# Index queries by halves of the tokens, two pairs of blocks that trade their counting engine, and a reordered start, in a two-layer decoder trunk

## The chip, the cores and the metric

The kernel runs on one core of one Trainium2 chip. The metric is the device time of one execution, in microseconds; the time shown is the median of several runs. Five engines matter: PE (TensorE), DVE (VectorE), ACT (ScalarE), POOL (GpSimd) and the sync queue SP, which issues nearly all DMAs.

## The reference

```python
# layer 0: sparse attention; layer 1: gated short convolution; each followed by a SwiGLU FFN
mod = silu(c) @ ada_w[i] + ada_b[i]                  # shifts, scales and gates, 6 x 1024
h = rmsnorm(x, norm1_g[i]) * (1 + sc1) + sh1
...
q, k, v, qi, ki, wi = split(h @ w_in)                # 16 heads, 4 kv heads, 8 index heads, dim 64
q, k = rope(rmsnorm(q)), rope(rmsnorm(k)); qi = rope(qi); ki = rope(layernorm(ki))
for each block of 128 queries:
    score = einsum(relu(einsum(qi, ki)), wi)         # summed over the 8 index heads
    score = where(causal, score, -inf)
    sel = top_k(score, 256)                          # 256 keys for every query
    p = softmax(q . k[sel] * scale); o = p . v[sel]
x = x + g1 * (o @ w_out)
x = x + g2 * swiglu(rmsnorm(x, norm2_g[i]) * (1 + sc2) + sh2)
```

1024 tokens, model width 1024, everything in float32. Blocks 0 and 1 (the first 256 queries) see at most 256 keys, so that only blocks 2 to 7 need scores and a selection.

## The kernel before

All instructions are recorded first and then ordered when the program is built: `Plan.drain` is a list scheduler. Each engine has a clock of its own; among the operations whose inputs are ready it issues the one with the lowest `pri`, which is a due time in microseconds set in the code that records the operation. `unit(s)` sets the due time `T_PROJ + s * SLOT` (45 + 6.2 s). Tiles with a tag live in rings, and a ring hands out its buffers in the order in which the program recorded them: a tile can't be had before the earlier tile in its buffer has been read for the last time. Each engine then runs its own list in order. All instructions are emitted at line 244, so that the rows below tell groups apart by tile names.

A product of float32 matrices is made of three matmuls on split operands: `split` makes a rounded high part (`whi`, `hhi`: a cast, on ACT mostly) and the remainder (`wlo`, `hlo`: a subtraction on DVE). `wpair` loads one pair of weight tiles (two `raw` loads of 512 KB) and splits it into the four units of the ring `whi`/`wlo`, four casts and four subtractions.

The start, `first_norm`: eight loads of x are transposed on PE into `xt`, through the PSUM ring `mm` of two banks. The shift and scale of layer 0 (`mod`, j = 0 and 1) come from 16 loads of 512 KB of `ada_w`, eight for each j (k = 0 to 7). Five eighths of each row block are summed on DVE (`ada_step`, tile `sc`), three eighths on PE (`ada_pe`): three one-column matmuls for a k, each k in a tile of its own of the ring `mm`, followed by a DVE addition into `mod`. The loads go to tiles `stage`, `raw` and `s4` (shown as `s`). `vectors` loads the small parameter vectors into rows, transposes them, and `ada_scale` needs its `norm1_g`. `rope_tables` needs its frequencies and makes C and S, which go through DRAM (`rd`). At the end `nz`, `hhi` and `hlo` are the normalized input.

`project`: KI (index key and weights) for both halves of 512 tokens; then the index queries QI: for each of two column pairs j, one `wpair`, and both halves (of half 0 only its last 256 tokens, as blocks 0 and 1 need none); `rope_pair` copies (`rt`), rotates (`sw`, `rt`) and writes to DRAM (`qid`). Then, for each block 2 to 7, `index` loads the block's queries back (`karena<-qid`), makes 4 x 2 score tiles on PE (`ps_L`), ACT takes their relu (`s`), and eight DVE operations add them up (`sc<-s,wiT,sc`). `select` finds the 256th largest score of two blocks at once bit by bit, 31 bits: a count of the scores above a trial value for each block (tile `junk`), then three small DVE operations on `bs`. The count is a Sign with an accumulator on ACT, or a compare with an accumulator on DVE. Before, blocks 2, 3 count on DVE, and 4, 5 and 6, 7 on ACT. The bits' due times run from the pair's start to `until[pair]`. `selected` then makes the block's mask `bias` by ten or so DVE operations. K, Q and V projections follow in the program (512-column matmuls into `mm`), and attention, `attend`, comes after the pools of the projection have been closed. It runs blocks 0 to 7 in turn, with the output projection and 48 more `ada_w` steps (`adaw`, `adacc`) between them.

Of the kernel before, what the change touches and what calls it, by code (L numbers as in the profile page):

```python
# [9 lines left out]
F32 = mybir.dt.float32  # L10
F32R = mybir.dt.float32r
BF16 = mybir.dt.bfloat16
# [3 lines left out]
ALU = mybir.AluOpType  # L16
# [434 lines left out]
P = 128  # L451
T = 1024
D = 1024
KT = D // P
TB = T // P
HW = 512
NH = 2
# [4 lines left out]
IH = 8  # L462
TOPK = min(256, T // 4)
FREE_BLK = TOPK // P
# [7 lines left out]
C_QI = C_V + KVH * HD  # L472
# [3 lines left out]
R_C, R_N1, R_N2, R_CW, R_G, R_IF = 0, 8, 24, 40, (64, 96), 66  # L476
# [6 lines left out]
def blk(b):  # L483
    return slice(b * P, (b + 1) * P)


class Trunk:
# [94 lines left out]
        nc.vector.tensor_tensor(out, r, t, op=ALU.mult)  # L582


    def setup(self, c, ada_b, arenas):
        nc, cp = self.nc, self.cp
        self.ident = ident = cp.tile([P, P], F32, name="ident")
        nc.gpsimd.memset(ident, 1.0)
        nc.gpsimd.affine_select(ident, ident, pattern=[[-1, P]], compare_op=ALU.is_equal,
                                fill=0.0, base=0, channel_multiplier=1)  # L590
        self.ones = cp.tile([P, 1], F32, name="ones")
        nc.vector.memset(self.ones, 1.0)
        self.blk4 = cp.tile([P, 4], F32, name="blk4")
        nc.vector.memset(self.blk4, 0.0)
        for i in range(4):
            nc.vector.memset(self.blk4[32 * i:32 * i + 32, i:i + 1], 1.0)
        rc, rowb = arenas[0].part_of(0)[0:8, P:2 * P], arenas[1].part_of(0)[0:96, 0:P]
        nc.sync.dma_start(rc, c.rearrange("o (k p) -> (o k) p", p=P))
        self.plan.pri = 1.2
        nc.sync.dma_start(rowb, ada_b.rearrange("l (k p) -> (l k) p", p=P))  # L600
        self.cact = cp.tile([P, 8], F32, name="cact")
        pv = self.ps("sm")
        nc.tensor.transpose(pv[:, 0:8], rc, ident[:8, :8])
        nc.scalar.activation(self.cact, pv[:, 0:8], AF.Silu)
        self.adab = cp.tile([P, 96], F32, name="adab")
        pb = self.ps("sm")
        nc.tensor.transpose(pb[:, 0:96], rowb, ident[:96, :96])
        nc.vector.tensor_copy(self.adab, pb[:, 0:96])
        mod = cp.tile([P, 2, 6, 8], F32, name="mod")
        self.mod = [[mod.part_of((i, j))[:, i, j] for j in range(6)] for i in range(2)]  # L610
        aff = cp.tile([P, 2, 2, 8], F32, name="aff")
        self.aff = [[aff.part_of((i, j))[:, i, j] for j in range(2)] for i in range(2)]

    def vectors(self, n1, n2, conv_w, gq, gk, lg, lb, rope_c, arenas, kgb):

        nc, cp = self.nc, self.cp
        rows = arenas[0].part_of(1)[:, 0:P]
        nc.vector.memset(rows, 0.0)
        for r0, n, v in ((R_N1, 16, n1.rearrange("l (k p) -> (l k) p", p=P)),
                         (R_N2, 16, n2.rearrange("l (k p) -> (l k) p", p=P)),  # L620
                         (R_CW, 24, conv_w.rearrange("o w (k p) -> (o w k) p", p=P)),
                         (R_IF, 1, rope_c)):
            nc.sync.dma_start(rows.part_of((1, r0))[r0:r0 + n, :], v)
        g = arenas[1].part_of(96)[96:98, 0:HD]
        for r, v in enumerate((gq, gk)):
            nc.sync.dma_start(g[r:r + 1], v)
        self.plan.pri = 1.15
# [6 lines left out]
        rd = [1] + [(1, r) for r in (R_N1, R_N2, R_CW, R_IF, *R_G)]  # L634
        nc.tensor.transpose(pv[:, 0:P], rows.part_of(rd), self.ident)
        nc.vector.tensor_copy(vec, pv[:, 0:P])
        self.plan.pri = 25.5
# [31 lines left out]
        if j in (1, 4) and c0 + n == KT or layer == 0 and j == 1:  # L669
            self.ada_scale(layer, j)  # L670

    def ada_pe(self, w, layer, j, k, d0, tag="mm"):


        n = w.free // P
        ps, dst, b0 = self.ps(tag), self.mod[layer][j][:, d0:d0 + n], layer * 48 + j * 8 + d0
        for d in range(n):
            self.nc.tensor.matmul(ps[:, d:d + 1], w[:, blk(d)], self.cact[:, k:k + 1],
                                  start=True, stop=True)
        self.nc.vector.tensor_tensor(dst, ps[:, 0:n], dst if k else self.adab[:, b0:b0 + n],  # L680
                                     op=ALU.add)

    def ada_scale(self, layer, j):

        n, r0 = (0, R_N1) if j == 1 else (1, R_N2)
        r0 += 8 * layer
        self.nc.vector.scalar_tensor_tensor(self.aff[layer][n], self.mod[layer][j], 1.0,
                                            self.vec[:, r0:r0 + 8], op0=ALU.add, op1=ALU.mult)

    def raw(self):  # L690
        return self.wp.tile([P, D], F32, name="raw", tag="raw")
# [76 lines left out]
def trunk_kernel(tc, x, c, positions, ada_w, ada_b, norm1_g, norm2_g, attn_w_in, attn_q_norm_g,  # L768
                 attn_k_norm_g, idx_k_ln_g, idx_k_ln_b, attn_w_out, conv_w_in, conv_w,
                 conv_w_out, ffn_w_gate, ffn_w_up, ffn_w_down, rope_c, out):  # L770
    plan = Plan(tc.nc, tc)
    with ExitStack() as ctx:
        ctx.enter_context(tc.manual_schedule())
        tk = Trunk(plan)
        for p in (tk.cp, tk.pp):
# [4 lines left out]
        a.first_norm(x, positions, lambda v: tk.setup(c, ada_b, v), lambda v: tk.vectors(  # L780
            norm1_g, norm2_g, conv_w, attn_q_norm_g, attn_k_norm_g, idx_k_ln_g, idx_k_ln_b,
            rope_c, v, a.score[2][:, 256:384]))
        a.project()
        a.attend()
# [22 lines left out]

class Attention:
    T_PROJ, SLOT = 45.0, 6.2
    ON_ACT = 4  # L810

    def __init__(self, tk, w, w_out, ada_w, xspill):
        self.tk, self.nc, self.w, self.w_out = tk, tk.nc, w, w_out
# [3 lines left out]
        def dram(name, shape):  # L817
# [19 lines left out]
        self.junk = [sel.tile([P, n], BF16, name="junk%d" % n) for n in (self.ON_ACT * P, T)]  # L837
# [13 lines left out]
    def first_norm(self, x, positions, setup, vectors):  # L851
# [9 lines left out]
        for tt in range(TB):  # L861
            plan.pri = 1.0 + tt
            h = tt // 4
# [4 lines left out]
            for i in range(2):  # L868
                ps = tk.ps()
# [8 lines left out]
            if tt % 4 == 3:  # L878
                bc = tk.norm_bc(ss.part_of(h)[:, 4 * h:4 * h + 4], sp, "L")[:, 0:HW]
                plan.pri = 5.0 + 4 * h  # L880
                for d in range(KT):
                    plan.tt(zs[h].part_of(d)[:, d], xT[h](d), bc, ALU.mult)
        plan.pri = 13.5
        vectors((self.C, self.S))
        for j in (1, 0):
            acc = self.score[5 + j][:, 0:5 * P]
            stage = self.hp.tile([P, 4, D], F32, name="stage%d" % j, tag="hi0" if j else "lo0")
            for k in range(KT):
                plan.pri = 10.0 + k + 8 * (1 - j)
                if k % 2:  # L890
                    w = stage.part_of(k)[:, k // 2]
                else:
                    w = self.s4() if k % 4 else tk.raw()
                last = nc.sync.dma_start(w, tk.ada_rows(self.ada_w, 0, j, k))
                plan.pri = 1.1
                tk.ada_step(w[:, 0:5 * P], k, acc)
                tk.ada_pe(w[:, 5 * P:], 0, j, k, 5)
            tk.ada_end(0, j, [acc])
        plan.pri = 28.5
        tk.rope_tables(positions, self.C, self.S, self.score[4:2:-1], self.rd)  # L900
        self.h = []
        for half in range(NH):
# [30 lines left out]
    def project(self):  # L933
# [13 lines left out]
            s += 1  # L947
        self.unit(s + 1)
        self.ki_chain(kw)
        for j in range(IH // 4):  # L950
            self.unit(s)
            w = tk.wpair(self.w, C_QI + j * 2 * P)
            for half in range(NH):
                ts = slice(max(0, FREE_BLK * P - half * HW), HW)
                ab, sl, s = self.rope_pair(w, half, ts, None, None, s)
                for two in range(2):
                    self.to_dram(ab[two], self.qid, j, two, half, sl)
        self.free_bias()
        t = s
        ends = []  # L960
        for n, b in enumerate(range(FREE_BLK, TB)):
            self.unit(t)
            self.index(b, n)
            t += 0.5
            if b % 2:
                self.unit(t)
                ends += self.select((b - 1, b), b >= self.ON_ACT)
        for pri, end, args in sorted(ends, key=lambda e: e[0]):
            plan.pri = pri
            end(*args)  # L970
# [25 lines left out]
        for b in range(TB):  # L996
            ps = tk.ps()[:, 0:KVH * HD]
            for k in range(KT):
                hi, lo = (v[:, blk(b % 4)] for v in self.h[b // 4](k))
                tk.mm3(ps, hi, lo, *w[k // 4](k % 4), k == 0, k == KT - 1)  # L1000
            plan.copy(self.vst.part_of(b)[:, b], ps)
            s += 0.5
            self.unit(s)

    def rope_pair(self, w, half, ts, col, ss, s):

# [102 lines left out]
    def index(self, b, n):  # L1109
# [1 line left out]
        wd = (b + 1) * P  # L1111
        q = self.karena.part_of((1 + n // 2, n % 2))[:, 1 + n // 2, half_of(n % 2)].rearrange(
            "p (h t) -> p h t", t=P)
        nc.sync.dma_start(q, self.qid[:, blk(b)].rearrange("(h p) t -> p h t", p=P))
        sc = self.score[b]
        for hp in range(IH // 2):
            rs = [self.s4()[:, 0:wd] for _ in range(2)]
# [720 lines left out]
```

## Time and profile before

| | us |
|---|---|
| median of 3 runs (2352.1 to 2356.06) | 2353.39 |
| the profiled execution | 2353.95 |
| its span in the trace | 2352.2 |

The profile and the trace show one execution. Times in rows are from the start of the span. 1.75 us of the execution's time lie outside the span.

### The profile page before, as it was taken

How to read it: one execution, taken by the hardware profiler on the slowest of the kernel's cores; microseconds unless marked ns; L12 is line 12 of the kernel's file. 1: busy time of each engine (PE TensorE's matmuls, PEld its weight loads, DVE VectorE, ACT ScalarE, POOL GpSimd, SP SyncE). 2: the span in 40 equal slices, each digit the busy share in tenths (PEclk: the TensorE clock that was granted, in tenths of full speed). 3: DMA queues.
4: the chain of work that ended last, by engine and by line, in shares of the span. 5: the costliest groups of instructions: out<-in, count | busy, mean ns of one | idle time of the engine just before them, and what ended most of it. 6: DMA issues, size and time to landing. Idle time of an engine off the chain costs nothing.

```text
span 2352.2 us, 32869 instructions
## 1 busy us (share of the span) xinstructions
PE 2263.6 (96%) x11743; PEld 1828.6 (78%) x11743; DVE 1887.3 (80%) x3858; ACT 1121.7 (48%) x2106; POOL 5.1 (0%) x19
## 2 busy tenths in 40 slices
PE   7999989999999999999999899999999999999999
PEld 6757866776797778888887677788878888888877
DVE  5789979686589888887699989886898766665996
ACT  4468989857754233333343552223553333333434
POOL 0000000000000000000000000000000000000000
PEclk7999999999999999999999999999999999999999
DMA  7414332322244756443944143334344222238343
GB/s 287 123 53 99 102 105 73 117 91 64 81 140 131 223 177 188 151 153 111 326 139 147 63 131 113 103 90 152 109 126 152 89 90 76 90 119 311 126 161 112
DMA packets 304078, 311.27 MB, mean 132 GB/s; under 512 B 15113, under 2 KB 208682, under 8 KB 303914
## 3 DMA queue, kind: packets, MB, share of 16 engines
q1 hardware_dynamic: 302474, 307.86, 41.1%
q8 instruction: 92, 1.51, 0.3%
q10 hardware_dynamic: 1440, 1.31, 0.2%
q14 instruction: 72, 0.59, 0.1%
HBM read 258.00 MB, written 51.12 MB: 131 GB/s over the span
## 4 chain that ended last, share of the span: by engine, by line
PE 74%; DVE 16%; DMA 6%; ACT 2%; issue 2%; SPq 0%; ACTq 0%; DVEq 0%
PE ps_g L244 38%; PE ps_mm L244 26%; PE ps_sm L244 5%; DVE u L244 2%; PE ps_L L244 2%; PE ps_o L244 2%; DVE wlo L244 2%; DVE sc L244 2%; DMA adaw<-in_ada_w_dram 2%; DVE v L244 2%; DVE s L244 2%; DVE xr L244 1%; ACT p L244 1%; DVE p L244 1%; DVE adacc L244 1%
## 5 line engine op out<-in xcount | busy, mean ns | idle before, releaser
L244 ACT CAST whi<-s 128x512 fp32r<-128x512 f32 x341 | 211.4, 621 | 457.9 <-PE ps_g L244 181.4
L244 PE MATMUL ps_g<-t,whi 128*128 128x512 f32 x1160 | 361.2, 392 | 3.8 <-ACT t L244 2.9
L244 ACT CAST whi<-raw 128x512 fp32r<-128x512 f32 (+1 forms) x271 | 165.9, 618 | 366.2 <-PE ps_g L244 145.5
L244 PE MATMUL ps_g<-h,whi 128*128 128x512 f32 x1080 | 333.9, 390 | 0.0
L244 DVE TENSOR_TENSOR wlo<-raw,whi 128x512 fp32r<-128x512 f32 (+1 forms) x288 | 195.8, 684 | 79.4 <-ACT whi L244 79.0
L244 PEld LDWEIGHTS ps_g<-t,whi 128*128 128x128 f32 x1160 | 218.3, 189 | 51.0 <-ACT t L244 3.3
L244 DVE TENSOR_TENSOR wlo<-s,whi 128x512 fp32r<-128x512 f32 x342 | 232.5, 684 | 26.4 <-ACT whi L244 25.8
L244 PEld LDWEIGHTS ps_g<-h,whi 128*128 128x128 f32 x1080 | 202.2, 188 | 41.6
L244 PE MATMUL ps_g<-t,wlo 128*128 128x512 f32 x580 | 227.6, 392 | 4.8 <-DVE wlo L244 4.7
L244 PE MATMUL ps_g<-ph,whi 128*128 128x512 f32 x660 | 207.6, 393 | 4.4 <-DVE ph L244 2.3
L244 PE MATMUL ps_g<-h,wlo 128*128 128x512 f32 x540 | 210.5, 390 | 0.0
L244 PE MATMUL ps_mm<-t,whi 128*128 128x512 f32 x632 | 198.9, 396 | 4.0 <-ACT whi L244 4.0
L244 PEld LDWEIGHTS ps_g<-ph,whi 128*128 128x128 f32 x660 | 125.3, 190 | 32.4 <-DVE ph L244 3.3
L244 PEld LDWEIGHTS ps_mm<-t,whi 128*128 128x128 f32 x632 | 120.8, 192 | 30.3 <-ACT whi L244 5.1
L244 PEld LDWEIGHTS ps_g<-t,wlo 128*128 128x128 f32 x580 | 109.4, 189 | 29.7 <-DVE wlo L244 7.1
L244 DVE CUSTOM_DVE_ANT_0 p<-ps_L,bias 128x512 f32<-128x512 f32 (+3 forms) x192 | 100.1, 551 | 38.9 <-PE ps_L L244 22.2
L244 PE MATMUL ps_g<-ph,wlo 128*128 128x512 f32 x330 | 130.5, 395 | 0.0
L244 PE MATMUL ps_mm<-t,wlo 128*128 128x512 f32 x316 | 125.3, 396 | 4.7 <-DVE wlo L244 4.6
L244 ACT ACTIVATE junk<-sc,bs 128x896 bf16<-128x896 f32 (+3 forms) x124 | 123.4, 995 | 8.4 <-DVE bs L244 6.6
L244 ACT ACTIVATE p<-p,nm,qsc 128x256 f32<-128x256 f32 (+7 forms) x128 | 113.2, 886 | 21.4 <-DVE nm L244 19.9
L244 DVE SCALAR_TENSOR_TENSOR adacc<-adaw,cact,adacc 128x512 f32<-128x512 f32 x140 | 104.4, 746 | 20.5 <-DMA adaw<-in_ada_w_dram 20.3
L244 PEld LDWEIGHTS ps_g<-h,wlo 128*128 128x128 f32 x540 | 101.4, 188 | 21.6 <-DVE wlo L244 0.4
(331 smaller groups left out, 4713.1 us busy)
## 6 DMA issues: line engine op xcount, KB each, us to landing
ph<-in_ffn_w_down_dram SPq DMA_DIRECT2D x88, 512.0 KB
adaw<-in_ada_w_dram SPq DMA_DIRECT2D x160, 256.0 KB
raw<-in_ffn_w_gate_dram SPq DMA_DIRECT2D x52, 512.0 KB
raw<-in_ffn_w_up_dram SPq DMA_DIRECT2D x52, 512.0 KB
rt<-hid SPq DMA_DIRECT2D x64, 256.0 KB
raw<-in_conv_w_in_dram SPq DMA_DIRECT2D x32, 512.0 KB
hid<-u SPq DMA_DIRECT2D x52, 256.0 KB
raw<-in_ffn_w_down_dram SPq DMA_DIRECT2D x44, 256.0 KB
```

The lines of the kernel that those rows point to most:

```text
L244: f(*[a.get() if isinstance(a, Ref) else a for a in args], **{k: a.get() if isinstance(a, Ref) else a for k, a in kw.items()})
```

## The change

Three groups of edits.

- Start: `norm1_g` is loaded with `c` and transposed with it, so that `ada_scale` for j = 1 needs no `vectors`; `vectors` is recorded after the `ada_w` steps, with the due time 28.5. `ada_pe` accumulates all eight k of a j in one PSUM bank of the ring `o`, and one DVE addition follows. The `ada_w` rows of j = 0 go to eight slots in the buffers that held x.
- Index queries: half 0 of both column pairs comes first, then half 1 of pair 1 (with the weights already there) and half 1 of pair 0, whose weights are loaded and split again. Blocks 2, 3 are indexed and their selection begun behind half 0; a block's query load depends on the parts of `qid` of its own half alone. A half of 256 columns counts for half a slot, so that all later due times of the projection are two slots (12.4) earlier.
- Counting: blocks 2, 3 and 6, 7 on ACT, 4, 5 on DVE.

```diff
-        rc, rowb = arenas[0].part_of(0)[0:8, P:2 * P], arenas[1].part_of(0)[0:96, 0:P]
-        nc.sync.dma_start(rc, c.rearrange("o (k p) -> (o k) p", p=P))
+        rc, rowb = arenas[0].part_of(0)[0:24, P:2 * P], arenas[1].part_of(0)[0:96, 0:P]
+        nc.sync.dma_start(rc[0:8], c.rearrange("o (k p) -> (o k) p", p=P))
+        nc.sync.dma_start(rc[8:24], n1.rearrange("l (k p) -> (l k) p", p=P))
...
-    def ada_pe(self, w, layer, j, k, d0, tag="mm"):
+    def ada_pe(self, w, k, ps):
         n = w.free // P
-        ps, dst, b0 = self.ps(tag), self.mod[layer][j][:, d0:d0 + n], layer * 48 + j * 8 + d0
         for d in range(n):
             self.nc.tensor.matmul(ps[:, d:d + 1], w[:, blk(d)], self.cact[:, k:k + 1],
-                                  start=True, stop=True)
-        self.nc.vector.tensor_tensor(dst, ps[:, 0:n], dst if k else self.adab[:, b0:b0 + n],
-                                     op=ALU.add)
+                                  start=k + d == 0, stop=k == KT - 1 and d == n - 1)
...
-        plan.pri = 13.5
-        vectors((self.C, self.S))
         for j in (1, 0):
             acc = self.score[5 + j][:, 0:5 * P]
-            stage = self.hp.tile([P, 4, D], F32, name="stage%d" % j, tag="hi0" if j else "lo0")
+            stage = [self.hp.tile([P, 4, D], F32, name="stage%d" % j, tag=tag)
+                     for tag in (("hi0",) if j else ("lo0", "lo1"))]
+            ps = tk.ps("o")
             for k in range(KT):
                 plan.pri = 10.0 + k + 8 * (1 - j)
-                if k % 2:
-                    w = stage.part_of(k)[:, k // 2]
+                if j == 0 or k % 2:
+                    w = stage[k // 4 if j == 0 else 0].part_of(k)[:, k % 4 if j == 0 else k // 2]
                 else:
                     w = self.s4() if k % 4 else tk.raw()
...
-                tk.ada_pe(w[:, 5 * P:], 0, j, k, 5)
+                tk.ada_pe(w[:, 5 * P:], k, ps)
+            nc.vector.tensor_tensor(tk.mod[0][j][:, 5:], ps[:, 0:3],
+                                    tk.adab[:, 8 * j + 5:8 * j + 8], op=ALU.add)
             tk.ada_end(0, j, [acc])
         plan.pri = 28.5
+        vectors((self.C, self.S))
...
-    ON_ACT = 4
+    ON_ACT, IDX = (2, 3, 6, 7), 0.5
...
-        for j in range(IH // 4):
+        ends = []
+        for half, j in ((0, 0), (0, 1), (1, 1), (1, 0)):
             self.unit(s)
-            w = tk.wpair(self.w, C_QI + j * 2 * P)
-            for half in range(NH):
-                ts = slice(max(0, FREE_BLK * P - half * HW), HW)
-                ab, sl, s = self.rope_pair(w, half, ts, None, None, s)
-                for two in range(2):
-                    self.to_dram(ab[two], self.qid, j, two, half, sl)
+            if (half, j) != (1, 1):
+                w = tk.wpair(self.w, C_QI + j * 2 * P)
+            ts = slice(max(0, FREE_BLK * P - half * HW), HW)
+            ab, sl, e = self.rope_pair(w, half, ts, None, None, s)
+            s += (e - s) * (ts.stop - ts.start) / HW
+            for two in range(2):
+                self.to_dram(ab[two], self.qid, j, two, half, sl)
+            if (half, j) == (0, 1):
+                ends += self.indexed(s, (2, 3))
         self.free_bias()
-        t = s
-        ends = []
-        for n, b in enumerate(range(FREE_BLK, TB)):
-            self.unit(t)
-            self.index(b, n)
-            t += 0.5
-            if b % 2:
-                self.unit(t)
-                ends += self.select((b - 1, b), b >= self.ON_ACT)
+        ends += self.indexed(s, (4, 5, 6, 7))
...
+    def indexed(self, t, blocks):
+        ends = []
+        for b in blocks:
+            self.unit(t)
+            self.index(b, b - FREE_BLK)
+            t += self.IDX
+            if b % 2:
+                self.unit(t)
+                ends += self.select((b - 1, b), b in self.ON_ACT)
+        return ends
...
-        nc.sync.dma_start(q, self.qid[:, blk(b)].rearrange("(h p) t -> p h t", p=P))
+        src = self.qid.part_of([(b // 4, j, two) for j in range(2) for two in range(2)])
+        nc.sync.dma_start(q, src[:, blk(b)].rearrange("(h p) t -> p h t", p=P))
```

## Rows read from the trace of the kernel before

**Rows 1.** Busy time of each engine by stretch: PE, PEld, DVE, ACT, POOL, clock, DMA

```profile
100.00:111.50 11.50, 11.50 (x55) 9.46 (x54) 5.63 (x11) 4.39 (x8) 0.00 (x0) 1.00 0.33 101
111.50:125.00 13.50, 10.28 (x45) 8.08 (x43) 4.66 (x7) 2.28 (x4) 0.00 (x0) 1.00 0.43 126
125.00:187.00 62.00, 60.62 (x270) 30.44 (x270) 58.69 (x125) 45.24 (x101) 3.03 (x5) 0.97 0.15 43
187.00:309.00 122.00, 121.97 (x702) 106.23 (x702) 115.05 (x438) 111.14 (x216) 0.29 (x1) 1.00 0.36 96
309.00:430.00 121.00, 107.02 (x896) 73.15 (x893) 99.66 (x384) 109.73 (x293) 0.00 (x0) 0.97 0.33 101
```

**Rows 2.** Chain that ended last, in order of time: start, us, what

```profile
107.81 3.68 PE ps_mm L244 x16
...
116.17 8.87 DMA karena<-qid
...
237.77 8.81 PE ps_mm L244 x38
...
308.98 4.39 DMA adaw<-in_ada_w_dram
...
339.37 0.81 ACT junk L244 x2
...
424.25 1.03 ACT junk L244 x2
```

**Rows 3.** Order of time in the start: start, us, engine, operation, [idle before]

```profile
25.23 0.83 PE L244 MATMUL ps_mm<-cact,raw 128*128 128x1 f32 x6
...
29.31 1.44 PE L244 MATMUL ps_mm<-cact,s 128*128 128x1 f32 x6 [2.41 <-DVE mod L244]
...
54.59 1.52 ACT L244 ACTIVATE nz<-zs,mod,aff 128x512 f32<-128x512 f32 x2 [1.67 <-DVE mod L244]
```

**Rows 4.** Busy time by stretch in the start, columns as in the first group

```profile
24.00:28.00 4.00, 2.70 (x21) 2.22 (x20) 3.71 (x6) 1.66 (x3) 0.00 (x0) 0.91 0.93 312
32.00:36.00 4.00, 4.00 (x21) 4.00 (x21) 1.42 (x9) 0.00 (x0) 0.00 (x0) 0.50 0.74 258
```

**Rows 5.** PE's busy time on tile ps_mm: stretch, length, busy (count), clock, DMA

```profile
111.50:125.00 13.50, 10.28 (x45) 1.00 0.43 126
125.00:140.00 15.00, 3.92 (x9) 0.89 0.25 71
140.00:160.00 20.00, 9.81 (x34) 1.00 0.09 28
160.00:187.00 27.00, 8.94 (x27) 1.00 0.13 39
```

**Rows 6.** Groups by shape, 0 to 330 us: count, busy us, mean ns, idle before

```profile
L244 PE MATMUL ps_L<-karena 64*128 64x512 f32 x96 | 26.2, 636 | 1.2 <-ACT s L244 1.0
...
L244 DVE TENSOR_TENSOR wlo<-raw,whi 128x512 fp32r<-128x512 f32 x36 | 24.4, 684 | 4.7 <-ACT whi L244 4.6
...
L244 ACT ACTIVATE junk<-sc,bs 128x768 bf16<-128x768 f32 x26 | 24.3, 936 | 0.5
...
L244 ACT ACTIVATE junk<-sc,bs 128x640 bf16<-128x640 f32 x26 | 21.5, 828 | 2.3 <-DVE bs L244 2.0
...
L244 DVE SCALAR_TENSOR_TENSOR sc<-s,wiT,sc 128x512 f32<-128x512 f32 x7 | 5.2, 739 | 0.1
...
L244 DVE SCALAR_TENSOR_TENSOR sc<-s,wiT,sc 128x384 f32<-128x384 f32 x7 | 4.3, 618 | 1.5 <-ACT s L244 1.0
...
L244 DVE TENSOR_SCALAR_CACHE_REDUCE junk<-sc 128x768 bf16<-128x768 f32 x1 | 0.9, 936 | 0.0
...
L244 DVE TENSOR_SCALAR_CACHE_REDUCE junk<-sc 128x640 bf16<-128x640 f32 x1 | 0.8, 812 | 0.0
```

**Rows 7.** Tile ps_L on PE, sum of the stretches from 57 to 309 us

```profile
sum 252.00, PE 36.53; mean PE 2.44
```

**Rows 8.** Tile ps_sm on PE, the same sum (160 matmuls)

```profile
sum 252.00, PE 19.48; mean PE 1.30
```

**Rows 9.** Tile junk (the counts), sum of stretches from 80 to 460 us

```profile
sum 380.00, DVE 47.55 ACT 132.49; mean DVE 2.50 ACT 6.97
```

**Rows 10.** Tile junk, sum of stretches from 300 to 700 us

```profile
sum 400.00, DVE 0.00 ACT 49.50; mean DVE 0.00 ACT 2.48
```

More of the change, by code (lines that the diff above doesn't have):

```diff
@@ L582, in rsqrt_small, with setup @@
         nc.vector.tensor_tensor(out, r, t, op=ALU.mult)
-    def setup(self, c, ada_b, arenas):
+    def setup(self, c, ada_b, n1, arenas):
         nc, cp = self.nc, self.cp
@@ L601, in setup @@
         self.cact = cp.tile([P, 8], F32, name="cact")
+        self.n1 = cp.tile([P, 16], F32, name="n1")
         pv = self.ps("sm")
-        nc.tensor.transpose(pv[:, 0:8], rc, ident[:8, :8])
+        nc.tensor.transpose(pv[:, 0:24], rc, ident[:24, :24])
         nc.scalar.activation(self.cact, pv[:, 0:8], AF.Silu)
+        nc.vector.tensor_copy(self.n1, pv[:, 8:24])
         self.adab = cp.tile([P, 96], F32, name="adab")
@@ L612, in setup, with vectors @@
         self.aff = [[aff.part_of((i, j))[:, i, j] for j in range(2)] for i in range(2)]
-    def vectors(self, n1, n2, conv_w, gq, gk, lg, lb, rope_c, arenas, kgb):
+    def vectors(self, n2, conv_w, gq, gk, lg, lb, rope_c, arenas, kgb):
         nc, cp = self.nc, self.cp
@@ L618, in vectors @@
         nc.vector.memset(rows, 0.0)
-        for r0, n, v in ((R_N1, 16, n1.rearrange("l (k p) -> (l k) p", p=P)),
-                         (R_N2, 16, n2.rearrange("l (k p) -> (l k) p", p=P)),
+        for r0, n, v in ((R_N2, 16, n2.rearrange("l (k p) -> (l k) p", p=P)),
                          (R_CW, 24, conv_w.rearrange("o w (k p) -> (o w k) p", p=P)),
@@ L626, in vectors @@
             nc.sync.dma_start(g[r:r + 1], v)
-        self.plan.pri = 1.15
         for i, r in enumerate(R_G):
@@ L633, in vectors @@
         pv = self.ps("sm")
-        rd = [1] + [(1, r) for r in (R_N1, R_N2, R_CW, R_IF, *R_G)]
+        rd = [1] + [(1, r) for r in (R_N2, R_CW, R_IF, *R_G)]
         nc.tensor.transpose(pv[:, 0:P], rows.part_of(rd), self.ident)
         nc.vector.tensor_copy(vec, pv[:, 0:P])
-        self.plan.pri = 25.5
         self.kgb = kgb.rearrange("p (a d) -> p a d", d=HD)
@@ L670, in ada_end @@
             self.ada_scale(layer, j)
-    def ada_pe(self, w, layer, j, k, d0, tag="mm"):
+    def ada_pe(self, w, k, ps):
         n = w.free // P
-        ps, dst, b0 = self.ps(tag), self.mod[layer][j][:, d0:d0 + n], layer * 48 + j * 8 + d0
         for d in range(n):
             self.nc.tensor.matmul(ps[:, d:d + 1], w[:, blk(d)], self.cact[:, k:k + 1],
-                                  start=True, stop=True)
-        self.nc.vector.tensor_tensor(dst, ps[:, 0:n], dst if k else self.adab[:, b0:b0 + n],
-                                     op=ALU.add)
+                                  start=k + d == 0, stop=k == KT - 1 and d == n - 1)
     def ada_scale(self, layer, j):
[L685 to L688, printed above, removed]
+        g = self.n1 if j == 1 else self.vec[:, R_N2:R_N2 + 16]
+        self.nc.vector.scalar_tensor_tensor(self.aff[layer][j == 4], self.mod[layer][j], 1.0,
+                                            g[:, 8 * layer:8 * layer + 8],
+                                            op0=ALU.add, op1=ALU.mult)
     def raw(self):
@@ L779, in trunk_kernel @@
         a = Attention(tk, attn_w_in[0], attn_w_out[0], ada_w, xspill)
-        a.first_norm(x, positions, lambda v: tk.setup(c, ada_b, v), lambda v: tk.vectors(
-            norm1_g, norm2_g, conv_w, attn_q_norm_g, attn_k_norm_g, idx_k_ln_g, idx_k_ln_b,
+        a.first_norm(x, positions, lambda v: tk.setup(c, ada_b, norm1_g, v), lambda v: tk.vectors(
+            norm2_g, conv_w, attn_q_norm_g, attn_k_norm_g, idx_k_ln_g, idx_k_ln_b,
             rope_c, v, a.score[2][:, 256:384]))
@@ L836, in __init__ @@
                                           for b in range(FREE_BLK, TB)]
-        self.junk = [sel.tile([P, n], BF16, name="junk%d" % n) for n in (self.ON_ACT * P, T)]
+        self.junk = [sel.tile([P, n], BF16, name="junk%d" % n) for n in (6 * P, T)]
         cum = np.cumsum([0] + [6.8 * (b + 1) for b in range(TB)])
```

## The prediction

> **What bounds the kernel now.** I first read the busy times of the engines by stretch [rows 1], then the chain that ended last in order of time [rows 2], then the start operation by operation [rows 3, 4]. The change touches only what comes before about 470 us; the feed-forward and convolution stages behind it keep their work. So the question is how much earlier attention begins, and whether attention gets shorter.
>
> The reader is to see four stages. In the start, until the first `nz` at 54.59, PE works through the `ada_w` steps: one step is 0.83 us at a granted clock of 0.91 and 1.44 us at 0.50 [rows 3, 4]. The first step comes right behind the last transposes of x at 25, though `ada_w` rows land earlier, since both share the two banks of the ring `mm`, handed out in program order; the third step sits idle for 2.41 us behind a DVE addition into `mod` [rows 3]. From the index queries' end at 111.49 to 187, PE runs the score tiles together with K. There DVE is the full engine, 58.69 of 62 us between 125 and 187, but before that it is nearly empty: 5.63 of 11.5 and 4.66 of 13.5 us [rows 1], while everything waits for the queries to come back from DRAM, 8.87 us on the chain [rows 2]. From 187 to 309 PE is the bound: 121.97 of 122 us busy, and the chain is PE at 8.81 us for 38 matmuls, 0.232 us each [rows 1, 2]. From 309 attention runs with no single bound: ACT 109.73, PE 107.02, DVE 99.66 of 121 us [rows 1]; the chain goes through waits for `adaw`, then ACT with seven pieces of counting in it (the first and the last in [rows 2], 6.9 us together), then PE and DVE in turn.
>
> **The change part by part.** I work against the profiled execution, 2353.95 us (span 2352.2 and 1.75 outside it), which is 0.56 above the median of 2353.39. About 0.2% (4.7 us) is what a measurement of this kernel can tell from no change.
>
> *The start.* Sixteen steps keep their matmuls; sixteen DVE additions into `mod` become two, and they hold PE no longer. With a bank of their own (`o`), the steps of j = 1 can slip between the transposes, where PE is idle 1.3 of 4 us [rows 4]. I count the 2.41 us of idle time and two steps at 1.44 us that leave the serial stretch behind 29 us: 2.41 + 2.88 = 5.3, taken as **-5**. The upper bound has four steps gone: 2.41 + 5.76 = 8.2. The loads of j = 0 no longer wait for a `raw` or `s4` buffer; with PE at the slow clock behind them this frees nothing more. `vectors` moves behind 16 `ada_w` loads on SP: seven or eight small loads leave the head of that queue, and the frequencies for the rotary tables arrive later. Nobody but `rope_tables` and later work waits for them, and the tables are made on DVE beside `nz` and `hlo`, so I cost the move at nothing; if the tables came late, the rotation of half 0, now the first thing that the scores of blocks 2, 3 wait for, would eat the gain of this part, so its other bound is 0. The added transpose of 24 rows in place of 8 and one copy are a few tenths under the wait for x.
>
> *The order of the index queries.* Matmuls are the same. Added is one `wpair`: 1 MB of loads, four casts, four subtractions of 0.684 us [rows 6], 2.7 us of DVE. ACT's four casts, on an engine with 7 of 11.5 us free [rows 1], are hidden, and so are the loads. What is not hidden: the four weight units are one ring, and two passes over half 0 with 256 columns are short, so the split of pair 1's units has to wait for pair 0's last reads. I take **+1.5** for it: one cast or subtraction with its hand-over in each of two changes of weights; bounds 0 and four subtractions in a row, 2.7.
>
> *Blocks 2, 3 early.* Fourteen additions of 0.618 and 0.739 us are 9.5 us [rows 6], with the two first ones about 10.5, of DVE. They move from the stretch in which DVE is full into the 100 to 125 us, where 14.7 us of it are free [rows 1]. Their query load hides behind half 1 of the queries; the load for block 4 still has the way through DRAM, but now scores of 2, 3 are there to run meanwhile. What that is worth is not DVE's 10.5 us but PE's slack, for PE bounds the next stage and its work does not shrink. From 111.5 to 187 PE has 115 matmuls [rows 5] at 0.232 = 26.7 us, score tiles of 36.5 [rows 7], 32 of the 160 small matmuls, 3.9 us [rows 8]: 67.1 of 75.5 us. So 8.4 us are slack, of which 3.2 are the plain gap before the queries arrive (13.5 - 10.28 [rows 1]). I take the gap and a third of the rest: **-5**, bounds 0 and -8.4.
>
> The Trainium skill (DMA: Bandwidth & Descriptors, section "Anatomy of one DMA") fits a DMA from the gpsimd queue as about 2.0 us plus its bytes at 436 GB/s, which would make an estimate of 2.6 us for a query block of 256 KB. The row has 8.87 us for a load on the sync queue, so the trace does not bear that figure out here; by the page PE's gap would be gone already, and the sum 3.2 us smaller.
>
> *Who counts.* A Sign of 768 takes 0.936 and of 640 0.828 us [rows 6], 0.108 per 128 columns, so 512 and 384 would take 0.72 and 0.61. Blocks 2, 3 in place of 4, 5 thus save ACT 31 x (1.764 - 1.33) = 13 us. ACT also begins earlier, in the 100 to 187 us where it idles 35 us [rows 1]. Of its counting, 49.5 us lie behind 300 us [rows 10]; with 13 less and some 15 of the idle time used, about 20 remain. Of the seven pieces on attention's chain I take half as gained: **-3.5**. The bounds: 0, and 121 - 107 = -14, where PE alone would set that stage. DVE pays: 31 x (0.812 + 0.936) = 54 us of counts [rows 6] for 47.55 less six first counts of some 0.87 each, 42.3 [rows 9]: 12 us more, with the splits 14.7. Between 187 and 309 it has 7 us free, from 100 to 125 4.2 after the scores; the other 3.5 fall behind 309, where 21 us are free [rows 1]. The need is later too: block 4 comes later than block 2. I cost it at nothing; without that cover it is a rival below. The due times that move up by 12.4 touch the projections alike and change little among them.
>
> The sum: -5 + 1.5 - 5 - 3.5 = -12, so 2353.95 - 12 = **2342 us**.
>
> **The rivals.** *Attention gives more.* If ACT's relief lets PE set the stage (-14) and the start and the slack give their bounds (-8.2, -8.4), the change is worth 30 us: 2324. For it: ACT is the busiest engine there; against: the chain shows PE and DVE taking turns with it. About 2330 is its middle.
>
> *PE is simply the bound.* The slack between 111.5 and 187 stays, as PE waits for other things (a score tile's bank, a relu behind a count in ACT's queue), attention goes through other waits of the same length, and the start gives 3: -3 + 1.5, 2352. For it: PE is 97% or more busy from 125 to 309; the counts of 2, 3 on ACT now stand between relus and copies in its list.
>
> *DVE becomes the bound, and it ends slower.* The 14.7 us extra don't find idle time: the list is fixed when the program is built, and a count in it stands before a rotation or `wlo` for which PE waits. Then the 14.7 come out at the end, less the start's 5: 2353.95 + 9.7 = 2364. It decides if the last count of blocks 4, 5 comes after the place where attention's block 4 is first masked, or if DVE has no idle time left between 187 and 309. For it: DVE is 94% busy there already; against: the counts have the latest due times of what is on DVE.
>
> **How the numbers follow.** The forecast with its three gains, 2333 to 2348: 0.50. More from attention: 0.20. PE-bound, within 0.2%: 0.16. DVE-bound, slower: 0.14. Faster is 0.70, same 0.16, slower 0.14. The range leaves out the far ends of the first and the last rival: 2323 to 2357.
>
> **What would show it.** The first `nz` near 49 in place of 54.59; the steps of j = 1 between the transposes; no idle stretch of PE before the score tiles of block 4; Sign counts of 512 and 384 columns from about 115 us on; the last `ps_mm` of V, before attention's `adaw` wait, near 300 in place of 309; counting on ACT behind that point about 20 us in place of 49.5; `junk` on DVE ending before block 4 is masked. I'd be wrong in a term if its stage kept its length, and wrong in sign if DVE showed up as what PE waits for between 187 and 309.

## The result, and the profile after

The changed kernel takes 2368.09 us, median of 4 runs (2367.47 to 2369.27), against 2353.11 (2352.1 to 2356.06) beside it: 1.0062 of the time before, 95% interval 1.0045 to 1.008. It is 15 us slower, where 12 us less were forecast. Its span is 2365.7 us, 13.5 more than before.

The first view is the busy time by stage of the changed kernel, columns as in [rows 1]. The stages are the start, the first `nz` to the last score tile, from there to the last tile of V, attention, and then 240 us of the second feed-forward layer; the short stretches are those with idle time or half clock.

```profile
24.00:28.00 4.00, 4.00 (x22) 4.00 (x21) 4.00 (x7) 1.76 (x3) 0.00 (x0) 0.50 1.03 410
20.00:53.30 33.30, 31.61 (x150) 31.38 (x150) 22.12 (x42) 6.91 (x14) 0.00 (x0) 0.50 0.76 268
76.00:100.00 24.00, 21.23 (x134) 19.16 (x133) 18.29 (x47) 7.95 (x16) 0.00 (x0) 0.86 0.57 146
135.00:141.00 6.00, 1.16 (x5) 0.56 (x6) 0.49 (x3) 1.19 (x4) 0.00 (x0) 0.76 0.55 162
141.00:145.00 4.00, 4.00 (x15) 2.86 (x12) 1.55 (x3) 2.95 (x8) 0.00 (x0) 0.51 0.18 43
53.30:192.50 139.20, 126.71 (x592) 82.59 (x592) 114.96 (x251) 88.81 (x191) 2.98 (x5) 0.92 0.32 91
192.50:316.40 123.90, 122.40 (x692) 105.93 (x692) 117.13 (x405) 101.93 (x213) 0.83 (x1) 0.99 0.37 99
1850.00:2090.00 240.00, 240.00 (x1050) 196.89 (x1050) 165.25 (x258) 79.39 (x133) 0.00 (x0) 1.00 0.27 84
```

The same stretches of the kernel before:

```profile
20.00:54.60 34.60, 29.63 (x151) 28.36 (x149) 24.91 (x60) 7.33 (x17) 0.00 (x0) 0.60 0.74 255
76.00:100.00 24.00, 23.50 (x163) 20.94 (x162) 18.53 (x46) 6.92 (x14) 0.00 (x0) 1.00 0.44 127
54.60:187.20 132.60, 122.45 (x587) 78.62 (x587) 108.20 (x231) 75.60 (x154) 3.03 (x5) 0.95 0.31 95
187.20:308.60 121.40, 121.37 (x696) 105.72 (x696) 114.85 (x438) 110.57 (x214) 0.29 (x1) 1.00 0.36 96
1850.00:2090.00 240.00, 240.00 (x1061) 198.72 (x1060) 167.44 (x263) 78.63 (x133) 0.00 (x0) 1.00 0.29 91
```

Two things are to be seen. From `nz` to the end of V the changed kernel needs 263.1 us where the kernel before needed 254.1: PE is busy for 249.1 us of it in place of 243.8, and idle for 14.0 in place of 10.2. And in the last row, far behind the change, PE is busy without a gap at full clock in both, but gets 1050 matmuls done in place of 1061: from the start of one to the start of the next it is 228.9 ns in place of 226.7. The output tiles end at 683.2, 2.1 us later than before (681.1); the other 11.3 us of the span are lost behind them, in stages whose instructions the change does not touch.

The chain that ended last in the changed kernel, answering [rows 2]:

```profile
129.20 7.51 DMA qid<-rt
136.85 3.03 DMA karena<-qid
139.93 2.50 PE ps_L L244 x8
...
223.43 14.83 DMA raw<-in_attn_w_in_dram
...
299.91 16.56 PE ps_mm L244 x146
...
316.79 4.54 DMA adaw<-in_ada_w_dram
```

The way of the queries through DRAM is still on the chain (a store `qid<-rt`, then the load `karena<-qid`), now for block 4; a load of weights, `raw`, has joined it; and attention's wait for `adaw` begins 7.8 us later than in [rows 2].

The start in order of time, answering [rows 3]:

```profile
19.53 1.28 PE L244 MATMUL ps_o<-cact,raw 128*128 128x1 f32 x6
20.67 1.42 PE L244 MATMUL ps_o<-cact,stage 128*128 128x1 f32 x6
...
27.53 1.28 PE L244 MATMUL ps_o<-cact,raw 128*128 128x1 f32 x6
...
53.32 0.81 ACT L244 ACTIVATE nz<-zs,mod,aff 128x512 f32<-128x512 f32 x1 [9.51 <-DVE mod L244]
```

The groups of counts by shape, 0 to 330 us, answering [rows 6]:

```profile
L244 ACT ACTIVATE junk<-sc,bs 128x512 bf16<-128x512 f32 x31 | 22.5, 727 | 0.5
...
L244 ACT ACTIVATE junk<-sc,bs 128x384 bf16<-128x384 f32 x31 | 19.2, 620 | 7.3 <-DVE bs L244 4.9 <-DVE sc L244 2.2
...
L244 DVE TENSOR_SCALAR_CACHE_REDUCE junk<-sc,bs 128x768 bf16<-128x768 f32 x28 | 28.2, 1006 | 0.0
L244 DVE TENSOR_SCALAR_CACHE_REDUCE junk<-sc,bs 128x640 bf16<-128x640 f32 x28 | 24.4, 871 | 0.1
```

And the sums of all counts, 80 to 460 and 300 to 700 us, answering [rows 9, 10]:

```profile
sum 380.00, DVE 64.00 ACT 121.08; mean DVE 4.00 ACT 7.57
...
sum 400.00, DVE 14.30 ACT 42.55; mean DVE 2.04 ACT 6.08
```

### The profile page after: what moved, and what is told of

Its sections match the earlier page's. It is cut to its first block, busy times and chain, and to the rows that moved or that the text cites. A ratio compares the mean times of both kernels' runs of the same rounds, so it can differ in the third digit from the quotient of the medians.

```text
span 2365.7 us, 32866 instructions
## 1 busy us (share of the span) xinstructions
PE 2283.9 (97%) x11743; PEld 1837.3 (78%) x11743; DVE 1895.8 (80%) x3833; ACT 1120.6 (47%) x2127; POOL 5.6 (0%) x19
## 4 chain that ended last, share of the span: by engine, by line
PE 76%; DVE 13%; issue 5%; DMA 4%; ACT 2%; SPq 0%; POOL 0%; DVEq 0%; ACTq 0%; POOLq 0%
PE ps_g L244 41%; PE ps_mm L244 25%; PE ps_sm L244 5%; PE ps_o L244 2%; PE ps_L L244 2%; DVE u L244 2%; DVE v L244 1%; DVE p L244 1%; DMA adaw<-in_ada_w_dram 1%; DVE wlo L244 1%; DVE xr L244 1%; DVE adacc L244 1%; DVE s L244 1%; DVE sc L244 1%; DMA raw<-in_attn_w_in_dram 1%
## 5 line engine op out<-in xcount | busy, mean ns | idle before, releaser
L244 ACT CAST whi<-raw 128x512 fp32r<-128x512 f32 (+1 forms) x281 | 171.9, 618 | 357.9 <-PE ps_g L244 142.8
L244 DVE TENSOR_TENSOR wlo<-s,whi 128x512 fp32r<-128x512 f32 x342 | 232.6, 684 | 29.5 <-ACT whi L244 29.2
L244 ACT ACTIVATE junk<-sc,bs 128x896 bf16<-128x896 f32 (+3 forms) x124 | 109.6, 884 | 15.0 <-DVE bs L244 10.5
```

What stands on the lines that cost most here:

```text
L244: f(*[a.get() if isinstance(a, Ref) else a for a in args], **{k: a.get() if isinstance(a, Ref) else a for k, a in kw.items()})
```

## The experiments

**Where the tail loses.** The compiled programs differ in one thing behind attention: `n1`, 64 bytes in each partition, stands in the pool `const` at the left end of SBUF, and each tile behind it on that side is 64 bytes further. `h11` went from 52704 to 52768; the weights `whi` on the right side stay at 212960. Modulo 256 both stood at 224; now `h11` stands at 32, 64 bytes past the weights.

`e1_realign`: the changed kernel with one 64-byte buffer fewer ahead of `h11`.

```
-        tmp = sp.tile([P, 16], F32, name="rst", tag="rst", bufs=2)
+        tmp = sp.tile([P, 16], F32, name="rst", tag="rst", bufs=1 if sp.name == "u" else 2)
```

> The changed kernel with one small buffer fewer in the pool ahead of the feed-forward operands, so that these operands stand at the SBUF addresses of the kernel before, 64 bytes lower; every instruction is kept. Theory of placement: the new 64-byte vector n1 moved the moving operands of the feed-forward and convolution matmuls, and a matmul of 512 columns went from 226.7 to 229 ns for it; here it is 226.7 again and the 11 us behind attention are back: 2357 (2355 to 2359). Rival, placement does not matter and the tail is slower for another reason (what runs beside it, the clock's history): 2368, period still 229.

`e2_pad64`: the kernel before with an unused tile.

```
         self.cact = cp.tile([P, 8], F32, name="cact")
+        cp.tile([P, 16], F32, name="pad")
```

> The kernel before with nothing but an unused 64-byte tile at the place where the changed kernel has n1. Theory of placement: the instructions are those of the kernel before, yet the matmuls behind attention take 229 ns in place of 226.7 and the time is 2364 (2362 to 2366). Rival: 2353, as before, period 226.7.

Measured: `e1_realign` 2358.96, ratio to before 1.0023 (1.0014 to 1.0032); `e2_pad64` 2363.03, 1.0044 (1.0027 to 1.0061), 10.0 us more than the 2352.99 beside it. The stretch from 1850 to 2090, first of `e1_realign`, then of `e2_pad64`:

```profile
1850.00:2090.00 240.00, 240.00 (x1060) 198.72 (x1060) 167.19 (x262) 80.28 (x136) 0.00 (x0) 1.00 0.29 89
```

```profile
1850.00:2090.00 240.00, 240.00 (x1050) 196.91 (x1049) 164.95 (x258) 79.51 (x133) 0.00 (x0) 1.00 0.28 86
```

1060 matmuls with the old place, 1050 with the new, whichever kernel it is. An unused tile costs 10 us. The place theory stands, its rival falls. The trace holds some 6900 matmuls of 512 columns behind attention; 2.2 ns on each would make 15 us, so about two thirds of that reaches the end. Where the rest is hidden is not shown.

`e4_map`: matmuls alone, with the weights and the moving operand at every pair of places (256 pairs, the places 32 bytes apart).

```
+COMBOS = [(s, m) for s in range(0, 128, 8) for m in range(0, 128, 8)]
...
+        for n, (s, m) in enumerate(COMBOS):
...
+            for k in range(12):
...
+                for j, (a, b) in enumerate(((hi, xh), (hi, xl), (lo, xh))):
+                    nc.tensor.matmul(ps, a, b, start=k + j == 0, stop=k == 11 and j == 2)
```

> Only matmuls: it leaves out the whole computation and writes a slice of the modulation weights to the output. 256 pairs of a place for the weights and a place for the moving operand, each in steps of 32 bytes over 512, with 36 matmuls of 512 columns for each pair in the order of the kernel. Theory of placement: 226.7 ns for pairs with the same remainder, 229 to 232 for the others, and the map says which remainder counts (64, 128 or 512). Rival: one number for all 256 pairs.

The view is the busy time by stretch (PE, PEld, ACT, POOL, clock, DMA), a stretch for each 36 matmuls; the moving operand is 0, 32, 64, 96 and, in the last row, 256 bytes past the weights:

```profile
249.05:257.23 8.18, 8.18 (x37) 6.76 (x36) 0.00 (x0) 0.00 (x0) 1.00 0.00 0
257.23:265.64 8.41, 8.41 (x38) 6.75 (x36) 0.00 (x0) 0.00 (x0) 1.00 0.00 0
265.64:273.89 8.25, 8.25 (x38) 6.76 (x36) 0.00 (x0) 0.00 (x0) 1.00 0.01 2
273.89:282.30 8.41, 8.41 (x37) 6.76 (x36) 0.00 (x0) 0.00 (x0) 1.00 0.00 0
...
182.18:190.36 8.18, 8.18 (x37) 6.76 (x36) 0.00 (x0) 0.00 (x0) 1.00 0.00 0
```

8.18 / 36 = 227.2 ns at 0 and 256; 229.2 at 64; 233.6 at 32 and 96. From start to start within a pair, its first three matmuls left out, the number follows the difference of the two places modulo 256 and not either place: 226.7 to 227.3 ns at 0, 228.8 to 228.9 at 64, and 232.6 to 234.4 at the other six (the very first pair, in which matmuls still took 427 ns, is left out too). The three matmuls of a group at 64 take 226, 229 and 232 ns in turn, as they do in the changed kernel.

`s_pad32`: the map foretells that 32 bytes cost more than 64.

```
+        cp.tile([P, 8], F32, name="pad")
```

> The kernel before with an unused tile of 32 bytes in place of the 64 of the earlier run. The map of matmuls alone gave 226.7 to 227 ns where the moving operand and the weights stand at the same place modulo 256 bytes, 228.8 where the moving operand is 64 bytes further, 233.3 where it is 32 further. If that holds in the kernel: 64 bytes cost 2.3 ns a matmul and some 10 us in all, 32 bytes cost 6.6 ns and so some 29: 2382 (2377 to 2388). Rival, any place but the old one costs the same: 2363; or the map does not carry over and 32 bytes cost nothing: 2353.

2385.17, ratio 1.0124 (1.0109 to 1.0139): 30.1 us more than the 2355.04 beside it, where 29 were expected. The same stretch, 233.3 ns from start to start:

```profile
1850.00:2090.00 240.00, 240.00 (x1030) 192.78 (x1030) 160.96 (x252) 77.19 (x129) 0.00 (x0) 1.00 0.27 84
```

`e3_right320`: the projections' operands, 64 past the weights in both kernels, moved to 0.

```
+        sel.tile([P, 80], F32, name="pad")
         self.score = [None] * FREE_BLK + [sel.tile([P, (b + 1) * P], F32, name="sc%d" % b)
```

> The kernel before with an unused 320-byte tile in the pool sel, which moves the operands of the projections and of the output tiles from 288 to 480 above a multiple of 512, where the weights stand. Theory of placement, if it is the remainder shared with the weights that counts: about 700 projection matmuls go from 229 to 226.7 ns and 768 of 256 columns in the output tiles from 117.5 to 113.3, so 1.6 + 3.2, some 5 us less: 2348 to 2351. Rival: 2353, both as before.

2354.97, ratio 1.0006 (0.9995 to 1.0018): nothing gained. The spacing within groups fell to 227 ns in the projections, as expected, but in the output tiles, with 256 columns, it rose from 113 to 119 ns to 120. From 640 to 681 us PE, busy throughout, did 351 matmuls before and 343 here:

```profile
640.00:681.00 41.00, 41.00 (x351) 41.00 (x350) 31.93 (x54) 20.32 (x34) 0.00 (x0) 1.00 0.34 100
640.00:681.00 41.00, 41.00 (x343) 40.91 (x342) 31.45 (x54) 19.36 (x32) 0.00 (x0) 1.00 0.34 103
```

What is best for 512 columns is not best for 256; the map was not made for those.

**What the parts do alone.** All further kernels keep the feed-forward operands at their old addresses.

`p_start`: the changed kernel's start; the queries, blocks and counting of before. `p_order`: the kernel before with the new loop over `(half, j)` and `indexed`, `ON_ACT = (4, 5, 6, 7)`. `p_swap`: the kernel before with

```
-    ON_ACT = 4
+    ON_ACT = (2, 3, 6, 7)
...
-                ends += self.select((b - 1, b), b >= self.ON_ACT)
+                ends += self.select((b - 1, b), b in self.ON_ACT)
```

> The start's part of the change alone (n1 in setup, vectors behind the first modulation rows, sums kept in one bank), with the feed-forward operands at their old addresses; index queries, early blocks and counting as before. The prediction's step: the first nz about 5 us earlier and 2348. Rival, from the changed kernel's trace, where the cosine and sine tables came late, PE stood idle 2.3 us at 80 to 85 and ran at half clock for some 7 us behind it: the start gives 1 to 2 and the late tables take 4 to 6, so 2356 (2355 to 2358).

> The new order of the index queries and the early indexing of blocks 2, 3 alone; VectorE counts 2, 3 and ScalarE 4, 5 as before, and the start and every address are as before. The prediction's step: 1.5 for the weight ring, less 5 for PE's slack, 2350. Rival, from the changed kernel's trace: PE still waits for the queries of block 4, 4.8 us in place of 3.3, and comes back at half clock, so nothing is gained and 1 to 5 us are lost: 2354 to 2358.

> Only who counts: blocks 2, 3 on ScalarE and 4, 5 on VectorE, all else as before. The prediction's step: 3.5 less, 2350. From the changed kernel's trace, where attention took 310.5 us from its first product to its last in place of 316.3: 6 less, 2347. Rival: VectorE's added 12 us push the projections: 2353 to 2360.

Measured, with the ratio to the kernel before and its interval in brackets: 2364.32 (1.0041, 1.0026 to 1.0056), 2372.72 (1.0075, 1.0058 to 1.0093) and 2378.61 (1.0104, 1.0087 to 1.0121). Each part alone loses, by 10, 19 and 25 us; none of these numbers was among those expected. `e1_realign`, which has all three, loses 6. So they don't add up.

The traces say where. A pair of blocks is counted, turned into a `bias`, and only then masked, on DVE, in front of attention's products. The view is a tile's operations, here the writes of `bias`: count, duration, first and last start, shapes. First the kernel before (blocks 4 and 5), then `p_order` (4 and 5), then `p_swap` (2 and 3):

```profile
L244 DVE SCALAR_TENSOR_TENSOR bias<-s,s x2: 816/883/950, 395.1 to 410.4; 128x640 bf16<-128x640 f32 x1, 128x768 bf16<-128x768 f32 x1
```

```profile
L244 DVE SCALAR_TENSOR_TENSOR bias<-s,s x2: 826/889/952, 409.0 to 422.8; 128x640 bf16<-128x640 f32 x1, 128x768 bf16<-128x768 f32 x1
```

```profile
L244 DVE SCALAR_TENSOR_TENSOR bias<-s,s x2: 555/624/693, 368.8 to 377.8; 128x384 bf16<-128x384 f32 x1, 128x512 bf16<-128x512 f32 x1
```

With them go PE's busy times, between 390 and 430 of the kernel before and then of `p_order`, and between 350 and 370 of `p_swap`:

```profile
390.00:430.00 40.00, 35.39 (x317) 26.26 (x317) 35.74 (x120) 33.01 (x75) 0.00 (x0) 1.00 0.31 93
390.00:430.00 40.00, 28.78 (x214) 19.06 (x211) 34.03 (x109) 26.26 (x58) 0.00 (x0) 0.83 0.22 67
```

```profile
350.00:370.00 20.00, 11.40 (x93) 7.93 (x91) 14.78 (x49) 15.28 (x42) 0.00 (x0) 0.79 0.38 112
```

In `p_order` block 4's `bias` comes 13.9 us later than before and attention's output tiles end 16 later (697.1). In `p_start` the `bias` comes at 403.5, 8.4 later, and the tiles end 6 later (687.4). In `p_swap` that of block 2 comes at 368.8 where the kernel before had it at 299.7. For `p_swap` the reason lies in the list: it gives ScalarE blocks 2, 3 without indexing them early, and their last Sign starts at 358.6. `p_order` leaves 4, 5 on ScalarE as before, and yet their last Sign starts at 393.8 in place of 380.0; why is not shown. In the changed kernel blocks 2, 3 have theirs at 324.6 and 348.3, and 4, 5 at 388.5 and 397.4.

`r_both`: the new order and the new counting, without the start.

> The new order of the queries with early blocks 2, 3 and the new counting together, without the start's part; addresses as before. Theory of the counts' end: a pair of blocks must be counted before attention masks its first block; the order alone let 4, 5 end late (last Sign at 394), the swap alone 2, 3 (at 359), together 2, 3 end near 309 and 4, 5 near 371, so the 19 and 25 us that each loses alone are gone: 2354 to 2359. Rival, losses add up: 2353 + 19 + 25 = 2397. The prediction's sum for these parts (1.5 - 5 - 3.5): 2346.

2355.70, 1.0002 (0.9992 to 1.0012): the losses of 19 and 25 us cancel. These two parts belong together, and together they are neutral. Against `e1_realign` at 1.0023 the start's part costs 0.21%, 5 us.

`r_until`: `p_start` with an earlier due time for the counts of blocks 4, 5.

```
-        self.until = {2: self.t_att[2], 4: self.t_att[4] + 10.0, 6: self.t_att[7]}
+        self.until = {2: self.t_att[2], 4: self.t_att[4], 6: self.t_att[7]}
```

> The start's part alone, as run before (2364), with the due time of the last count of blocks 4, 5 set 10 us earlier. Theory of the counts' end: the 10 us were lost because ScalarE's last Sign of blocks 4, 5 came at 391 in place of 380, with block 4 waiting for its mask; with the earlier due time they come before 382 and the time is 2354 (2351 to 2357). Rival, the start's own part costs the 10 us: 2364.

A miss: 2374.31, 1.0085 (1.0069 to 1.01). The counts did not end sooner: the last Sign of block 5 came at 394.2 (391.1 in `p_start`), the `bias` of block 4 at 407.9, and PE then stood idle 9.2 us, until 410.7, for block 4's mask. That the mask waits for the counts is seen once more. An earlier due time did not make them end earlier; this is one trace, and why they came later is not shown.

**The start, the wait for queries, attention's first wait.**

`p_novec`: `e1_realign` with `vectors` called ahead of the modulation steps, as before.

```
+        plan.pri = 13.5
+        vectors((self.C, self.S))
         for j in (1, 0):
...
         plan.pri = 28.5
-        vectors((self.C, self.S))
```

> The changed kernel with its feed-forward operands at their old addresses, and with the small vectors loaded ahead of the modulation rows again, as in the kernel before. If the late tables are what the start costs: no idle stretch and no half clock at 80 to 90, so 4 to 6 us less than the 2359 of the same kernel with late vectors: 2354. Rival (the prediction costed the move at nothing): 2359.

2360.51, 1.0026 (1.0017 to 1.0035): no gain. Half the expectation held. From 76 to 100 PE is at 0.93 and busy 22.14 us (`e1_realign` 0.79 and 21.87) and V ends at 311.8 in place of 317.1, but the output tiles end at 683.1 in both. What is won ahead of attention is lost in it.

`s_bank`: `r_both` with the modulation steps on PE summed in a bank of their own, and nothing else of the start.

```
+            ps = tk.ps("o")
...
-                tk.ada_pe(w[:, 5 * P:], 0, j, k, 5)
+                tk.ada_pe(w[:, 5 * P:], k, ps)
+            nc.vector.tensor_tensor(tk.mod[0][j][:, 5:], ps[:, 0:3],
+                                    tk.adab[:, 8 * j + 5:8 * j + 8], op=ALU.add)
```

> The new order of the queries and the new counting together (2356 as run before), and of the start's part only that the modulation steps on PE have a bank of their own and are summed in it; n1 and the small vectors are loaded as in the kernel before. If the bank is what the start loses by (PE runs steps and transposes at half clock from 20 us on and meets the projections' start with no more than half clock): 2359 to 2361. Rival, the bank is neutral and the loads' order costs the 5 us: 2355.

2366.72, 1.0046 (1.0029 to 1.0062): more than the whole start costs. The bank does what it should at first, with `nz` at 50.8 where `r_both` has 53.4, but V ends at 316.4 in place of 308.6 and attention's output tiles at 690.3 in place of 679.9.

`r_kfirst`: `e1_realign` with

```
-        ends += self.indexed(s, (4, 5, 6, 7))
+        ends += self.indexed(s + 1.0, (4, 5, 6, 7))
```

`r_adagate`: `e1_realign` with attention's first modulation step behind the first mask, which `gate` is:

```
+        self.plan.gate = gate
         self.tk.ada_step(w, k, self.acc)
+        self.plan.gate = None
```

`s_gate`: the same edit on `r_both`.

> The changed kernel with its feed-forward operands at their old addresses, and the indexing of blocks 4 to 7 due one unit (6.2 us) later, so that tiles of K can run while the queries of block 4 come back from DRAM. Theory of the wait and the clock: PE's 4.8 us of idle time at 135 and the 7 us at half clock behind it go, V ends 5 to 8 us earlier: 2352 to 2355. Rival, the counts set attention's end and an earlier start of it is lost again: 2359.

> The changed kernel with its feed-forward operands at their old addresses, and the first modulation step of attention behind the first masked products in place of ahead of them on VectorE. It waits for a load that is issued only when the projections' buffers are free, and the masks stand behind it for 4.8 us. If attention's own start is what counts: 4 to 5 us less than 2359, 2354. Rival, the counts set attention's end: 2359.

> The new order of the queries and the new counting together (2356), with the first modulation step of attention behind the first masked products on VectorE. PE stood idle 5.4 us at 309 there and was 93% busy in attention behind it. If attention is bound by PE now: 4 to 5 us less, 2351. Rival, other waits take the place: 2356 or more, as the same edit on the changed kernel gave 9 us more.

2371.85 (1.0072, 1.0055 to 1.0089), 2367.62 (1.0055, 1.0043 to 1.0067) and 2356.34 (1.0006, 0.9997 to 1.0015): no gain in any. The first two even lose some 12 and 8 us against `e1_realign` (1.0023), which none of their theories had. `r_kfirst` did not remove the wait for block 4's queries (4.4 us at 135). In `r_adagate` the idle time at attention's start shrank to pieces, yet attention took 373.6 us from its first product to the last output tile, where `e1_realign` took 366.0. No version beats the kernel before. `r_both` and `s_gate` equal it within their intervals, and so beat the changed kernel.

## Why the prediction was wrong

**The step that failed** is the first one: that the feed-forward and convolution stages "keep their work" and so their time, and that the added transpose and copy for `n1` are "a few tenths". The work stayed; each matmul of 512 columns became 1% longer, 228.9 ns in place of 226.7, because the tile for `n1` shifts the moving operands against the weights. That is 9 to 10 of the 15 us, shown from both sides: `e1_realign` takes the shift away and gains 9.1 us on the changed kernel, `e2_pad64` puts it into the kernel before and loses 10.0. `e4_map` gives the pattern, and `s_pad32` came out as forecast from it. The prediction looked for costs in instructions and waits and had no term for an address. The Trainium skill (TensorE: Matmul & The Clock Gate, section "Step-by-step: what each phase is for") gives a gap of about 216 ns between matmuls of 512 columns. No run here shows less than 226.7 as a steady spacing for these operands, and in these runs it depends on where they stand.

The rest, some 5 to 6 us, is the schedule, where -12 were forecast:

- **The start, -5: nothing.** The steps did slip between the transposes, but PE was at 0.50, the lower of its two levels (1.2 GHz), from 20 to 53 us, and all sixteen took 1.28 to 1.42 us; before, only the first two took 0.83 [rows 3] and the others 1.28 to 1.44. The clock was 0.60 there before, with PE busy for 29.63 of 34.6 us, now 31.61 of 33.3: the gaps that were closed went into slower matmuls. The first `nz` stands at 52.3 to 54.6 us, mean 53.1, in the eight traces with the old start, and at 51.8 to 54.6, mean 53.2, in the six with the whole new one.
- **The vectors, 0:** wrong for their stage, right for the total. PE lost 2.3 us of busy time and 0.14 of the clock between 76 and 100; `p_novec` got some of it back, and the end did not move.
- **The weight ring and PE's slack, +1.5 and -5:** the slack was not used. PE stood idle 4.8 us for block 4's queries and came back at half clock (0.51 from 141 to 145). V ended at 316.4; I had said near 300. The wait alone does not explain it: `r_both` stands idle 5.6 us at that place and ends V at 308.6. From `nz` to V's end PE is idle 3.8 us longer than before and busy 5.3 us longer, at a mean clock of 0.92 in place of 0.95 in the first of the two stages. The 14.83 us of `raw` on the chain are the time of that load; PE itself waited 1.4 us near there, at 240.7, for ACT. I had taken the 8.87 us in [rows 2] as the way through DRAM; after, store and load are apart, 7.51 and 3.03. The estimate of 2.6 us for one DMA of this size, from the Trainium skill (DMA: Bandwidth & Descriptors, section "Anatomy of one DMA"), is near the load's 3.03; the store ahead of it took 7.51.
- **Who counts, -3.5:** attention took 366.8 us from its first product to the last output tile in place of 372.5, but it also began 7.8 us later, and `r_both`, with the same counting and attention's old beginning (308.5), took 371.4; so a gain of the counting is not shown. The prices of Sign held, 0.727 and 0.620 us for the 0.72 and 0.61 worked out, and ScalarE's counting fell by 11.4 us where 13 were forecast. VectorE's rose by 16.5 where 12 were: it was priced by the first count of a block, 0.936 and 0.812, and the others took 1.006 and 0.871. But I had treated counting as load that one engine is relieved of. It is a chain of 31 rounds that must end before a mask; the swap alone loses 25 us, as blocks 2 and 3 then come too late, although ScalarE's load falls by the same amount. With 42.55 us of counting on ScalarE behind 300 us, where I had said 20, it was not relieved as far either.
- **VectorE's extra work, 0:** the condition held in the changed kernel, whose last count of blocks 4, 5 starts at 370.9 us, ahead of their `bias`.

Of the rivals, "PE is simply the bound" at 2352 comes nearest for the schedule: `r_both`, without the start's part, is close to that case, with the slack unused and no gain. "DVE becomes the bound" gave 2364, near the result, by another road: its condition did not come true.

**What stays open:** why the start's part costs 5 us in company with the other two, and `s_bank` 11. The order of instructions differs in both from the start on, and V ends 8 us later in both. From `nz` to there PE is busy for 242.7 us and idle for 12.5 in `r_both`, 251.0 and 14.4 in `e1_realign`, 247.6 and 18.0 in `s_bank`: in part idle time, in part slower matmuls. The address of `n1` shifts attention's operands too, in `e1_realign` as well, but `e2_pad64` has the same shift and ends attention's output tiles at 677.7, where the kernel before has 681.1; that trace shows no loss from it. Executions of one list differ by 2 to 3 us in the start alone, and behind attention's output tiles single traces of kernels with the old feed-forward addresses took from 1671 to 1683 us, so a single trace does not settle 5 us. I can't name one cause.

## What to carry to other kernels

Compare the addresses of matmul operands before and after any new tile: here the difference of moving operand and weights modulo 256 bytes decided 1 to 3% of every matmul with 512 columns, and a tile of 64 or 32 bytes moved it. Where instructions that a change does not touch run slower at full clock, count them in a stretch in which the engine is full: 1061 against 1050 is seen at once. And a selection that has to be done before a mask is costed by when its last round ends, not by whose time it uses; parts that move that end are to be judged together.

## What the runs showed that was not expected

- The spacing of matmuls with 512 columns and 4-byte operands at full clock depends on the address of the moving operand less that of the weights, modulo 256 bytes: 227 ns at 0, 229 at 64, 233 to 234 at 32, 96 and the other multiples of 32 in a loop of matmuls, and the same at 0, 64 and 32 in the kernel.
- With 256 columns it is the other way round for the two places seen: 120 ns at 0, 113 to 119 at 64.
- An unused tile of 32 bytes costs this kernel 30 us, one of 64 bytes 10.
- A due time 10 us earlier went with counts of blocks 4, 5 that ended 3 us later, in one trace of each kernel.
